# Recurrence gate blocks as Strassen pairs, and recurrence heads moved ahead of the memory gates

## The chip, the cores and the metric

The kernel runs on one core of one Trainium2 chip. The time is device microseconds of one execution, from start to end on the core. Inside a core, TensorE (PE) multiplies matrices into PSUM banks, VectorE (DVE) and ScalarE (ACT) work elementwise, GpSimd (POOL) does small elementwise work, SyncE (SP) issues the loads and stores. Each engine takes its own queue of instructions in order and waits on semaphores for the others.

## The reference, cut to what matters

One decoder layer over 512 prompt tokens and 64 sample tokens (576 columns), with model width 1024 and float32 values. A normalised input `h` is projected by `w_in`; three branches (a convolution module, a gated linear recurrence with 4 heads, a cross attention into memory) are each projected to width 1024 and merged with a sigmoid gate per channel; an output projection and an FFN follow.

```python
z = jnp.einsum('bld,de->ble', h, w_in)
ca, cb, hq, hf, hi, hgate, mq, gl = jnp.split(z, idx, axis=-1)
...
logf = jnp.log(lbh + (1.0 - lbh) * jax.nn.sigmoid(fx))          # fx: hf by heads
k = (1.0 - lbh) * jax.nn.sigmoid(-fx)
q = jax.nn.silu(hq)
o, new_hg = _hgrn2_chunkwise(q, k, v, logf, hg_state)           # 4 heads, 128 x 128 state
o = _rmsnorm(o, hg_norm_g) * jax.nn.silu(hgate)
p_hg = jnp.einsum('ble,ed->bld', o, w_hg_out)
...
g = jax.nn.sigmoid(gl.reshape(B, L, N_BRANCH, D_MODEL))
merged = g[:, :, 0] * p_conv + g[:, :, 1] * p_hg + g[:, :, 2] * p_mem
out = jnp.einsum('bld,de->ble', merged, w_out)
```

## The kernel before

Activations lie transposed: 128 channels on the partitions, 576 tokens along a row. Every float32 product is done as three matmuls on split operands (`mm3`, L95 to L97: high by high, high by low, low by high). `split` (L102, L103) makes the high part on ACT and the low part on DVE. A block of 128 output channels (`proj`) is two groups of tokens, 256 and 320 columns, with 8 contraction steps of three matmuls for each: 48 matmuls, each group in a PSUM bank of its own. The tag `mm` has four banks, the tag `sd` four more for the recurrence and other small products.

The mixer is a list of tasks, added with `add` and run in that order. Each task computes one block, and after it `pump` advances the queues of side work by some steps: `convq` (convolution) and `side` (the recurrence of a head, among others). The weights of a block are loaded and split by `wprep`, some blocks ahead (`wahead`). The code sets program order; a scheduler then places each instruction in its engine's queue by its own estimate of when operands and buffers are free, so matmuls of a block and of a head alternate on PE. Buffers of a pool are handed out in program order: the tag `tb` (`tmp`) has three, which serve the squares of a head, its output before the split, and the gates of the memory branch among others.

The blocks around the change: `gate_conv`, `gate_mem` and `gate_hg` are 8 blocks of 48 matmuls each, evicted by a sigmoid on ACT (`gate_block`, L511). `p_conv`, `p_mem` and `p_hg` are 8 blocks each of 24 matmuls, evicted on DVE with a product by the gate (`out_block`, L517 to L521). `hq` and `hf` are the projections of one recurrence head. The order in before: the gate `hgate(0)`, head 0, the other `hgate`, 8 times `p_conv`, then the memory gates and `p_mem` in turns, with head 1 after `p_mem(1)` and head 2 after `p_mem(5)`, then `gate_hg(0)`, head 3, the other `gate_hg`, and 8 times `p_hg`.

A head is a chain over four engines: `hg_decay` (scans, a reciprocal L794, scaled keys; transposes L826 and L829, copied by ACT at L827 and L830), then `hg_main` (state products L847 with L853 on DVE; scores L871 to L878; new sample states L884; outputs L887, L890, L896, L898; squares on ACT L903 and L906; their sum on DVE L904; a reciprocal root on POOL in 14 small instructions, L144 to L153; scaling on DVE L909 and L911; transposes L915 and L916; the product with the head's gate L922 and L923; the split; state updates L933).

The FFN already forms blocks of two by Strassen products in Winograd's form: it halves tokens and contraction, forms sums of token blocks and of weight blocks (`token_sums_a`, `token_sums_b`, `sprep`), and gets a block of 256 channels with 7 products (`sprod`, 4 steps of `mm3` with 288 columns) in place of 8.

## Time and profile before

| what | before |
|---|---|
| median of 3 runs | 1005.29 us (1005.02 to 1006.93) |
| profiled execution, its time | 1005.55 us |
| its span | 1003.8 us |
| TensorE granted clock, mean share of full speed | 0.997 |
| PE busy | 986.9 us, 98%, 6915 instructions |
| DVE busy | 693.3 us, 69%, 1235 instructions |
| ACT busy | 433.5 us, 43%, 766 instructions |
| POOL busy | 33.5 us, 3%, 127 instructions |

The busy shares are means over stages that differ, and the windows of the stages in question are shown below. A row of a timeline gives start and length in us, then the instruction with its line; in brackets stands the idle time of that engine ahead of it and who ended it. `x4` means four instructions of a kind in a row, with the time from the first one's start to the last one's end. A buffer's name is the tag of its pool: `wr`, `wh`, `wl` are raw, high and low weights, `tn` the small tiles of the reciprocal root.

### The profile page before, as it was taken

What the parts mean: (1) busy time and instruction counts of PE and PEld (TensorE: products, weight loads), DVE (VectorE), ACT (ScalarE), POOL (GpSimd) and SP (SyncE); (2) the same over time, 40 slices, a digit from 0 to 9 for tenths busy, and PEclk for the clock granted to TensorE, in tenths of its full rate; (3) what the DMA queues carried; (4) which work ended last, traced back from release to release, by engine and by line L of the source; (5) the groups of instructions that cost most, each with busy time, mean ns of one, the idle gap of its engine ahead of it and who ended that gap; (6) DMA issues with size and microseconds to landing.
All of it is one profiled execution on the core that took longest, in us unless ns stands there. A gap on an engine that the chain in (4) does not pass through costs nothing.

```text
span 1003.8 us, 16880 instructions
## 1 busy us (share of the span) xinstructions
PE 986.9 (98%) x6915; PEld 924.0 (92%) x6915; DVE 693.3 (69%) x1235; ACT 433.5 (43%) x766; POOL 33.5 (3%) x127
## 2 busy tenths in 40 slices
PE   8999999999899999999999999999999999999997
PEld 7997899889699999999999779999999999999995
DVE  6689997485875365566548788878777876813715
ACT  6544346574621232223234466344444544614612
POOL 1120000000101001001000000000000000000000
PEclk9999999999999999999999999999999999999999
DMA  8415421543743222222323615023232333321302
GB/s 244 140 64 194 121 80 47 148 132 107 207 134 95 84 85 75 76 87 65 95 77 134 181 64 178 1 85 114 77 104 85 96 115 137 139 81 54 128 20 95
DMA packets 125931, 106.55 MB, mean 106 GB/s; under 512 B 3208, under 2 KB 110244, under 8 KB 125846
## 3 DMA queue, kind: packets, MB, share of 16 engines
q1 hardware_dynamic: 125854, 105.48, 33.9%
q8 instruction: 54, 0.88, 0.4%
q14 instruction: 23, 0.19, 0.1%
HBM read 97.15 MB, written 8.68 MB: 105 GB/s over the span
## 4 chain that ended last, share of the span: by engine, by line
PE 82%; DVE 7%; DMA 5%; ACT 2%; issue 2%; POOL 1%; SPq 0%; DVEq 0%; ACTq 0%
PE mm L96 18%; PE mm L95 18%; PE mm L97 18%; PE sd L96 3%; PE sd L95 3%; PE sd L97 3%; PE sd L1465 2%; PE sd L1466 2%; PE sd L1467 2%; DVE wl L103 1%; DMA x<-in_cache_mem_v_dram 1%; DMA wr<-in_w_ffn_gate_dram 1%; DVE S L428 1%; DMA wr<-in_w_out_dram 1%; DVE S L106 1%
## 5 line engine op out<-in xcount | busy, mean ns | idle before, releaser
L96 PE MATMUL mm<-S,wh 128*128 128x320 f32 (+1 forms) x1216 | 363.3, 299 | 0.3 <-DVE S L106 0.3
L95 PE MATMUL mm<-S,wh 128*128 128x320 f32 (+1 forms) x1216 | 361.5, 299 | 1.5 <-ACT S L105 1.0
L97 PE MATMUL mm<-S,wl 128*128 128x320 f32 (+1 forms) x1216 | 362.4, 299 | 0.0
L95 PEld LDWEIGHTS mm<-S,wh 128*128 128x128 f32 x1216 | 227.9, 188 | 6.5 <-issue 2.6
L97 PEld LDWEIGHTS mm<-S,wl 128*128 128x128 f32 x1216 | 228.3, 188 | 3.9 <-issue 3.5
L96 PEld LDWEIGHTS mm<-S,wh 128*128 128x128 f32 x1216 | 228.6, 188 | 3.6 <-issue 1.5
L103 DVE TENSOR_TENSOR wl<-wr,wh 128x1024 fp32r<-128x1024 f32 x98 | 119.6, 1221 | 127.9 <-ACT wh L102 127.5
L102 ACT ACTIVATE wh<-wr 128x1024 fp32r<-128x1024 f32 x98 | 103.6, 1059 | 224.9 <-PE mm L96 174.1
L428 DVE SCALAR_TENSOR_TENSOR S<-S,cT,S 128x512 f32<-128x512 f32 x120 | 89.9, 749 | 2.5
L96 PE MATMUL mm<-S,wq 128*128 128x288 f32 x216 | 63.7, 295 | 0.0
L97 PE MATMUL mm<-S,wq 128*128 128x288 f32 x216 | 63.7, 295 | 0.0
L96 PE MATMUL sd<-S,wq 128*128 128x288 f32 x216 | 63.6, 295 | 0.0
L95 PE MATMUL sd<-S,wq 128*128 128x288 f32 x216 | 63.6, 294 | 0.0
L95 PE MATMUL mm<-S,wq 128*128 128x288 f32 x216 | 63.6, 294 | 0.0
L97 PE MATMUL sd<-S,wq 128*128 128x288 f32 x216 | 63.1, 294 | 0.0
L102 ACT ACTIVATE wq<-ws 128x1024 fp32r<-128x1024 f32 x36 | 37.9, 1056 | 37.8 <-PE mm L96 35.2
L103 DVE TENSOR_TENSOR wq<-ws,wq 128x1024 fp32r<-128x1024 f32 x36 | 43.7, 1217 | 3.0 <-ACT wq L102 3.0
L103 DVE TENSOR_TENSOR S<-S,S 128x1152 fp32r<-128x1152 f32 (+3 forms) x46 | 44.1, 986 | 1.8 <-ACT S L102 1.7
L102 ACT ACTIVATE S<-S 128x1152 fp32r<-128x1152 f32 (+3 forms) x46 | 38.1, 864 | 6.9 <-DVE S L521 4.9
L97 PEld LDWEIGHTS mm<-S,wq 128*128 128x128 f32 x216 | 40.6, 188 | 0.0
L96 PEld LDWEIGHTS sd<-S,wq 128*128 128x128 f32 x216 | 40.5, 188 | 0.0
L95 PEld LDWEIGHTS sd<-S,wq 128*128 128x128 f32 x216 | 40.5, 188 | 0.0
(371 smaller groups left out, 1689.5 us busy)
## 6 DMA issues: line engine op xcount, KB each, us to landing
wr<-in_w_in_dram SPq DMA_DIRECT2D x52, 512.0 KB
wr<-in_w_ffn_down_dram SPq DMA_DIRECT2D x22, 512.0 KB
S<-in_w_ffn_gate_dram SPq DMA_DIRECT2D x9, 1024.0 KB
S<-in_w_ffn_up_dram SPq DMA_DIRECT2D x9, 1024.0 KB
x<-in_x_prompt_dram SPq DMA_DIRECT2D x8, 512.0 KB
wr<-in_w_mem_kv_dram SPq DMA_DIRECT2D x8, 512.0 KB
x<-in_cache_mem_k_dram SPq DMA_DIRECT2D x8, 512.0 KB
x<-in_cache_mem_v_dram SPq DMA_DIRECT2D x8, 512.0 KB
```

The source lines that it names most:

```text
L95: T.matmul(out, lhsT=whi, rhs=xhi, start=start, stop=False, skip_group_check=more)
L96: T.matmul(out, lhsT=whi, rhs=xlo, start=False, stop=False, skip_group_check=more)
L97: last["mm"] = T.matmul(out, lhsT=wlo, rhs=xhi, start=False, stop=stop, skip_group_check=more)
L102: A.activation(hi, src, AF.Copy)
L103: (eng or V).tensor_tensor(lo, src, f32(hi), op=ALU.subtract)
L106: ins2 = V.scalar_tensor_tensor(out=lo, in0=src, scalar=scale, in1=f32(hi), op0=ALU.mult, op1=ALU.subtract)
L428: queue(V.scalar_tensor_tensor(out=dp, in0=src, scalar=w, in1=dp, op0=ALU.mult, op1=ALU.add))
L1465: T.matmul(pa[ti], lhsT=ah, rhs=w[0][:, kk, :], start=f == 0, stop=False)
L1466: T.matmul(pa[ti], lhsT=al, rhs=w[0][:, kk, :], start=False, stop=False)
L1467: T.matmul(pa[ti], lhsT=ah, rhs=w[1][:, kk, :], start=False, stop=f == NF - 1)
```

## The change

There are three parts.

1. The eight `gate_hg` blocks become four pairs. A pair takes 7 products of 12 matmuls of 288 columns, and its weights come in one load of 1 MB with `sprep` (one split of 512 columns, four sums of 512, three splits of 1024). The token sums are formed once in `token_sums`: two additions of 2304 columns, four of 1152, four splits of 1152. The results of a pair are put together from held products (`hold_` on ACT, three per pair), three instructions of DVE and sigmoids on ACT.
2. The heads move. Head 1 stands ahead of `p_conv(0)`, head 2 after `p_conv(3)`, head 3 between `gate_mem(1)` and `p_mem(0)`. `token_sums` follows `p_mem(3)`, the first weights of the pairs (`first_sums`) follow `gate_mem(7)`, the four pairs and then `p_hg` end the list.
3. `hg_alloc` takes one large tile for all heads. Heads 1 and 3 keep `z`, `kx` and `q` in the convolution buffer `ca`.

The helpers of the FFN (`half`, `token_sums_a`, `token_sums_b`, `sprep`, `sprod`, `hold_`) move up in the code and take their operands as arguments; the FFN's work is the same as before. The diff, cut to its core:

```diff
     def hg_alloc(j):
-        s1, d = big(), {}
-        for i, key in enumerate(("z", "P", "R", "iP", "kx", "qT", "sc", "q")):
+        if j == 0:
+            hg["s1"] = big()
+        s1, d = hg["s1"], {}
+        for i, key in enumerate(("P", "R", "iP", "qT", "sc")):
             d[key] = s1[:, NT * i:NT * i + NT]
+        for i, key in enumerate(("z", "kx", "q")):
+            d[key] = ca[:, i] if j % 2 else s1[:, NT * (5 + i):NT * (6 + i)]
...
+    def token_sums_a(act, r):
+        hi, lo = (x[:, :, TH[0]] for x in act)
+        V.tensor_tensor(r[:, :, TH[0]], f32(hi), f32(lo), op=ALU.add)
...
+    def token_sums_b(x):
+        r = x["r"]
+        hi, lo = (a[:, :, TH[1]] for a in x["act"])
+        V.tensor_tensor(r[:, :, TH[1]], f32(hi), f32(lo), op=ALU.add)
+        b11, b12, b21, b22 = (r[:, 4 * k:4 * k + 4, TH[t]] for k in range(2) for t in range(2))
+        V.tensor_tensor(b11, b11, b12, op=ALU.subtract)
+        split(*x["T"][0], b11)
+        V.scalar_tensor_tensor(out=b12, in0=b12, scalar=-1.0, in1=b22, op0=ALU.mult, op1=ALU.add)
+        V.scalar_tensor_tensor(out=b22, in0=b22, scalar=-1.0, in1=b11, op0=ALU.mult, op1=ALU.subtract)
+        split(*x["T"][1], b22)
+        split(*x["T"][2], b12)
+        V.scalar_tensor_tensor(out=b21, in0=b22, scalar=-1.0, in1=b21, op0=ALU.mult, op1=ALU.subtract)
+        split(*x["T"][3], b21)
...
+    def gmul(key, x, nxt, g):
+        d = sw.pop(key)
+        act, T4 = x["act"], x["T"]
+        X, Z, Y = mmb(), sdb(), sdb()
+        sprod(X, d["a"], half(act, 0, 0), True)
+        c1 = hold_(X)
+        next(nxt, None)
+        sprod(Z, d["cd"], T4[0], True)
+        c5 = hold_(Z)
+        next(nxt, None)
+        sprod(X, d["acd"], T4[1], False)
+        u2 = hold_(X)
+        sprod(Y, d["b"], half(act, 1, 0), True)
+        V.tensor_tensor(g[:, 0, TH[0]], Y[:, :HT], c1, op=ALU.add)
...
-    def gate_hg(n):
+    def gprep(p):
+        c = C_GL + D + 256 * p
+        return sprep(p, w_in[0][:, c:c + 256], gring)
+
+    def token_sums():
+        wahead(3)
+        drain(side)
+        gring["t"] = big()
+        gx.update(token_sums_a(h, gring["t"].rearrange("p (k t) -> p k t", k=8)))
+        token_sums_b(gx)
+
+    def first_sums():
+        wahead(1)
+        for _ in gprep(0):
+            pass
+
+    def gates_hg(p):
...
+            nxt = gprep(p + 1) if p < 3 else iter(())
...
+            gmul(p, gx, nxt, G1["all"][:, 2 * p:2 * p + 2])
...
+    hf(1)
     for n in range(8):
         add(p_conv(n), *([wcols(w_conv_out, P * n, 256)] if n % 2 == 0 else []), conv=2, ns=3)
+        if n == 3:
+            hf(2)
     for n in range(0, 8, 2):
         add(gate_mem(n), win(C_GL + 2 * D + P * n), ns=4)
         add(gate_mem(n + 1), win(C_GL + 2 * D + P * n + P), ns=4)
+        if n == 0:
+            hf(3)
+        if n == 6:
+            add(first_sums, ns=0)
         add(p_mem(n), wcols(w_mem_out, P * n, 256), ns=3)
         add(p_mem(n + 1), ns=3)
-        if n == 0:
-            hf(1)
-        if n == 4:
-            hf(2)
+        if n == 2:
+            add(token_sums, ns=0)
+    for p in range(4):
+        add(gates_hg(p), ns=0)
     for n in range(8):
-        add(gate_hg(n), win(C_GL + D + P * n), ns=3)
-        if n == 0:
-            hf(3)
-    for n in range(8):
-        add(p_hg(n), *([wcols(w_hg_out, P * n, 256)] if n % 2 == 0 else []))
+        add(p_hg(n))
```

The lines of a head lie 6 further down in the changed kernel: L826 is L832 there, L898 is L904, L904 is L910, L909 is L915, L915 is L921.

Three places of the new order follow. The first is the third head on PE. Before, from its output products (L887) to its last transposes (L915), with the matmuls of two `gate_hg` blocks (`mm_4732` to `mm_4817`) between; rows of the same kind are left out:

```order
L887 MATMUL sd_4596<-S_1142,S_4279 64x128
L890 MATMUL sd_4596<-x_4508,qpad 32x128 x8
L896 MATMUL sd_4606<-S_1142,S_4279 128x128 x2
L898 MATMUL sd_4606<-S_1142,S_4279 128x128
...
L96 MATMUL mm_4732<-S_114,wh_4567 128x256
L97 MATMUL mm_4732<-S_113,wl_4568 128x256
L95 MATMUL mm_4757<-S_113,wh_4567 128x320
...
L915 MATMUL sd_4678<-ident,S_4279 128x128 x4
L916 MATMUL sd_4679<-ident,S_4279 128x64
```

And after, where `mm_4062` is the last block of `gate_mem(1)` and `mm_4096` the first of `hq(3)`:

```order
L97 MATMUL mm_4062<-S_113,wl_3890 128x320
L832 MATMUL sd_3765<-ident,S_2747 128x128 x4
...
L893 MATMUL sd_3848<-S_1142,S_2747 64x128
L896 MATMUL sd_3848<-x_3819,qpad 32x128 x8
L902 MATMUL sd_3893<-S_1142,S_2747 128x128 x2
L904 MATMUL sd_3893<-S_1142,S_2747 128x128
...
L921 MATMUL sd_3927<-ident,S_2747 128x128 x4
L922 MATMUL sd_3928<-ident,S_2747 128x64
L95 MATMUL mm_4096<-S_113,wh_4032 128x256
```

About 70 matmuls of blocks stood between the output products and the last transposes; now none does, nor between the first transposes and the last.

The second is ACT around the same head. Before, from the copy of the transposes (L827) to the first eviction behind the squares:

```order
L827 ACTIVATE S_4279<-sd_4483 128x512
L830 ACTIVATE S_1142<-sd_4489 64x128
L102 ACTIVATE wh_4786<-wr_4784 128x1024
L511 ACTIVATE tb_4512<-mm_4513 128x256
L511 ACTIVATE tb_4512<-mm_4538 128x320
L903 ACTIVATE tb_4616<-sd_4606 128x512
L906 ACTIVATE tb_4619,tn_4614<-sd_4596 64x128
L511 ACTIVATE S_4731<-mm_4732 128x256
```

After, where `mm_3978` to `mm_4062` are the four banks of `gate_mem(0)` and `gate_mem(1)`:

```order
L102 ACTIVATE wh_4152<-wr_4150 128x1024
L833 ACTIVATE S_2747<-sd_3765 128x512
L836 ACTIVATE S_1142<-sd_3771 64x128
L909 ACTIVATE tb_3903<-sd_3893 128x512
L912 ACTIVATE tb_3906,tn_3901<-sd_3848 64x128
L511 ACTIVATE tb_3977<-mm_3978 128x256
L511 ACTIVATE tb_3977<-mm_4003 128x320
L511 ACTIVATE tb_4036<-mm_4037 128x256
L511 ACTIVATE tb_4036<-mm_4062 128x320
```

The evictions of the gate blocks stood ahead of the head's squares; now four of them stand behind.

The third is DVE in the last head. Before, from the last state update to the product with the gate:

```order
L933 SCALAR_TENSOR_TENSOR x_5076<-x_5076,S_4790,sd_5102 128x128
L904 TENSOR_REDUCE tn_5181<-tb_5183 128x4
L909 TENSOR_TENSOR S_4790<-sd_5173,tn_5189 128x512
L911 TENSOR_SCALAR S_4790<-sd_5105,tn_5189 64x128
L103 TENSOR_TENSOR wl_5399<-wr_5396,wh_5398 128x1024
L922 SCALAR_TENSOR_TENSOR tb_5214<-sd_5207,cT,S_183 128x512
```

After, where `S_4622` holds the token sums:

```order
L939 SCALAR_TENSOR_TENSOR x_4334<-x_4334,S_2747,sd_4360 128x128
L957 TENSOR_TENSOR S_4622<-S_113,S_114 128x8x288
L964 TENSOR_TENSOR S_4622<-S_113,S_114 128x8x288
L910 TENSOR_REDUCE tn_4440<-tb_4442 128x4
L103 TENSOR_TENSOR wl_4619<-wr_4616,wh_4618 128x1024
L966 TENSOR_TENSOR S_4622<-S_4622 128x4x288
L968 SCALAR_TENSOR_TENSOR S_4622<-S_4622 128x4x288
L915 TENSOR_TENSOR S_2747<-sd_4432,tn_4448 128x512
L917 TENSOR_SCALAR S_183<-sd_4363,tn_4448 64x128
L969 SCALAR_TENSOR_TENSOR S_4622<-S_4622 128x4x288
L928 SCALAR_TENSOR_TENSOR tb_4473<-sd_4466,cT,S_183 128x512
```

Two additions of 2304 columns now stand ahead of the reduction, and a weight split and two token sums between it and the scaling.

## Rows read from the trace of the kernel before

**Rows 1.** Windows: length, busy us of PE, PEld, DVE, ACT, POOL, clock, DMA

```profile
286.00:520.00 234.00, 234.00 (x1808) 223.36 (x1806) 129.53 (x244) 58.64 (x106) 16.71 (x64) 1.00 0.26 80
325.00:350.00 25.00, 25.00 (x191) 25.00 (x190) 8.35 (x14) 6.08 (x10) 0.00 (x0) 1.00 0.28 85
640.00:850.00 210.00, 210.00 (x1585) 210.00 (x1585) 166.75 (x253) 99.19 (x155) 0.00 (x0) 1.00 0.29 95
371.10:396.65 25.55, 25.55 (x207) 23.13 (x206) 13.21 (x31) 5.52 (x12) 3.86 (x15) 1.00 0.29 86
```

**Rows 2.** Windows, second head, PE alone, matmuls into tile mm

```profile
371.10:396.65 25.55, 16.51 (x119) 1.00 0.29 86
```

**Rows 3.** Timeline of PE, second head: start, length, instruction, idle before

```profile
371.10 0.63 PE L826 MATMUL sd<-ident,S 128*128 128x128 f32 x4
...
374.86 1.06 PE L847 MATMUL sd<-S,S 128*128 128x128 f32 x8
...
379.10 0.33 PE L878 MATMUL sd<-S 128*64 128x64 f32 x2
...
382.17 1.13 PE L884 MATMUL sd<-tb,S 32*128 32x512 f32 x4
...
386.02 0.39 PE L898 MATMUL sd<-S,S 128*128 128x128 f32 x2
...
396.06 0.60 PE L915 MATMUL sd<-ident,S 128*128 128x128 f32 x4
```

**Rows 4.** Timeline of ACT, second head

```profile
371.76 0.60 ACT L827 ACTIVATE S<-sd 128x512 f32<-128x512 f32 x1 [2.76 <-PE sd L826]
...
374.91 1.06 ACT L102 ACTIVATE wh<-wr 128x1024 fp32r<-128x1024 f32 x1 [2.25 <-PE mm L96]
...
375.99 0.71 ACT L511 ACTIVATE tb<-mm 128x256 f32<-128x256 f32 x2
...
386.45 0.60 ACT L903 ACTIVATE tb<-sd 128x512 f32<-128x512 f32 x1 [9.74 <-PE sd L898]
```

**Rows 5.** Timeline of DVE, last head

```profile
500.50 0.69 DVE L904 TENSOR_REDUCE tn<-tb 128x4 f32<-128x512 f32 x1 [0.28 <-ACT tb L903]
505.20 0.69 DVE L909 TENSOR_TENSOR S<-sd,tn 128x512 f32<-128x512 f32 x1 [4.02 <-POOL tn L153]
```

**Rows 6.** Groups of DVE, 286 to 520: busy, mean ns | idle before

```profile
L794 DVE RECIPROCAL S<-S 128x576 f32<-128x576 f32 x3 | 11.2, 3725 | 0.0
...
L796 DVE SCALAR_TENSOR_TENSOR S<-S,omlb 128x576 f32<-128x576 f32 x3 | 2.4, 814 | 0.0
...
L922 DVE SCALAR_TENSOR_TENSOR tb<-sd,cT,S 128x512 f32<-128x512 f32 x4 | 3.0, 751 | 7.6 <-PE sd L915 7.6
```

**Rows 7.** Groups of DVE, 605 to 620 us: an addition of 2304 columns

```profile
L1223 DVE TENSOR_TENSOR S<-S,S 128x2304 f32<-128x2304 f32 x1 | 2.5, 2547 | 0.0
```

**Rows 8.** Groups of DVE and ACT, 640 to 860: pieces of 1152 columns

```profile
L103 DVE TENSOR_TENSOR S<-S,S 128x1152 fp32r<-128x1152 f32 x5 | 6.6, 1354 | 0.6 <-ACT S L102 0.6
...
L102 ACT ACTIVATE S<-S 128x1152 fp32r<-128x1152 f32 x6 | 6.6, 1155 | 0.2 <-DVE wq L103 0.2
```

**Rows 9.** Timeline of POOL and DVE, third head

```profile
452.26 1.23 DVE L103 TENSOR_TENSOR wl<-wr,wh 128x1024 fp32r<-128x1024 f32 x1 [3.37 <-ACT wh L102]
...
452.37 1.17 POOL L152 TENSOR_SCALAR tn<-tn 128x5 f32<-128x5 f32 x1
```

**Rows 10.** Chain that ended last: start, length, a load of weights

```profile
558.88 6.28 DMA wr<-in_w_ffn_gate_dram
```

**Rows 11.** Windows around the one drop of the clock, columns as in 1

```profile
256.00:258.20 2.20, 0.95 (x5) 0.59 (x4) 0.89 (x4) 2.20 (x7) 0.00 (x0) 1.00 0.16 48
258.20:262.00 3.80, 3.08 (x48) 2.49 (x52) 3.80 (x10) 3.24 (x5) 0.00 (x0) 0.67 0.39 119
262.00:266.00 4.00, 3.02 (x43) 2.30 (x36) 3.96 (x9) 4.00 (x9) 0.00 (x0) 0.88 1.14 318
```

More of the change, by code (lines that the diff above doesn't have):

```diff
@@ new lines, in sprod, with hold_ @@
+    def sprod(ps, w, x, start):
+        for k in range(4):
+            mm3(ps[:, :HT], w[0][:, k], w[1][:, k], x[0][:, k], x[1][:, k], start and k == 0, k == 3, not start)
+    def hold_(ps):
+        t = tmp(HT)
+        A.activation(t, ps[:, :HT], AF.Copy)
+        return t
+    def gmul(key, x, nxt, g):
[12 more added lines that the diff above has]
+        V.tensor_tensor(g[:, 0, TH[0]], Y[:, :HT], c1, op=ALU.add)
+        next(nxt, None)
+        sprod(X, d["ac"], T4[2], False)
+        o = g[:, 1, TH[1]]
+        V.scalar_tensor_tensor(out=o, in0=X[:, :HT], scalar=-1.0, in1=c5, op0=ALU.mult, op1=ALU.subtract)
+        A.activation(o, o, AF.Sigmoid)
+        next(nxt, None)
+        sprod(Z, d["abcd"], half(act, 1, 1), False)
+        V.tensor_tensor(g[:, 0, TH[1]], Z[:, :HT], u2, op=ALU.add)
+        A.activation(g[:, 0], g[:, 0], AF.Sigmoid)
+        next(nxt, None)
+        sprod(X, d["d"], T4[3], False)
+        A.activation(g[:, 1, TH[0]], X[:, :HT], AF.Sigmoid, scale=-1.0)
@@ L1288, in sprod @@
-    def sprod(ps, w, x, start):
-        for k in range(4):
-            mm3(ps[:, :HT], w[0][:, k], w[1][:, k], x[0][:, k], x[1][:, k], start and k == 0, k == 3, not start)
     def smul(m, nxt):
@@ L1295, in smul @@
         d = sw.pop(m)
-        T4 = [tuple(x[:, i] for x in xT["hl"]) for i in range(4)]
+        T4 = xT["T"]
         h0, h1 = hid(2 * p), hid(2 * p + 1)
@@ L1318, in smul @@
         u2 = hold_(X)
[L1319 removed]
+        sprod(Y, d["b"], half(h2, 1, 0), True)
         V.tensor_tensor(o0, Y[:, :HT], c1, op=ALU.add)
```

143 lines of the change are left out of this document (63 added, 80 removed).

## The prediction

> **What bounds the kernel now.** I read the busy shares first, then windows cut to the stretches that the change touches, then the timeline of one recurrence head on each engine. TensorE (PE) is the bound: between 286 and 520 us, where the memory gates, the recurrence heads and the gate_hg blocks lie, it is busy for 234.00 us of 234.00, while VectorE (DVE) is at 129.53 and ScalarE (ACT) at 58.64 [rows 1]. So there is no idle time that the new order could win back there. What can be won is PE work, and what can be lost is cover: a head is a chain over PE, ACT, DVE and GpSimd (POOL), and in the program of before PE fills each pause of that chain with matmuls of gate blocks and projections. In the second head's window of 25.55 us, 119 of PE's matmuls belong to such blocks [rows 2], so the pauses cost nothing. The question is whether the pauses are still filled.
>
> **The products: less PE work.** Eight gate blocks of 48 matmuls (24 of 256 columns, 24 of 320) are 384; four pairs of 7 products of 4 steps of 3 matmuls, 288 columns each, are 336. So 48 go. A matmul costs 25.00 / 191 = 131 ns in a stretch of plain blocks, whose mean is 288 columns, and 210.00 / 1585 = 132 ns in the stage that already uses such products in the FFN [rows 1]. The gain is 48 x 0.131 = **-6.3 us**, and it needs PE to be the bound in the new stage too. The FFN stage says that it is: PE is busy for 210.00 us of 210.00 and DVE for 166.75 with more work per pair than here [rows 1]. A pair of gates takes PE 84 x 0.132 = 11.1 us; DVE's splits, sums and three additions per pair come to less, since the FFN's also multiply the two branches. I take the added DVE and ACT work of the pairs at nothing, covered by these products; rival B prices the loss of that cover. ScalarE's sigmoid work stays about as it was.
>
> **A head without filler.** The second head in the trace gives the steps of the chain. Transposes begin at 371.10, and ACT's copy of 0.60 begins 0.66 later [rows 3, 4]. A split of 1.06 [rows 4] can stand ahead of the copy; I count about two thirds of it, and the first product L847 is ready 1.95 us after the start. L847 to the end of L878 is 379.43 - 374.86 = 4.6 us, less a little overlap 4.45, so 6.4. L884 to the end of L898 is 386.41 - 382.17 = 4.24 [rows 3], with a handover 10.8. Squares on ACT 0.60 [rows 4], 11.45; then the reduction on DVE, the reciprocal root on POOL and the scaling on DVE, which in the last head of before run from 500.50 to 505.89: 5.39, of which DVE waits 4.02 for POOL [rows 5]. That is 16.85; the transposes L915 and L916 add 0.55 [rows 3], 17.4 us in all. How much of a head does PE cost before? The window of 25.55 us less 119 matmuls of 0.131 (15.6): 10.0 us [rows 1, 2].
>
> **The third head: +7.4.** In the new order its PE rows, from the transposes to L922, stand in one piece with no projection among them; the next matmul is the first of the block hq(3). What keeps other blocks away is that the evictions of gate_mem(0) and gate_mem(1) on ACT, which free the four banks that hq(3) needs, stand behind this head's squares. So the chain is bare: 17.4 - 10.0 = +7.4. The evictions after the squares take 0.71 for two [rows 4] and end long before the chain, so they add nothing. If ACT has no split ahead it is 6.4, and if DVE still has weight parts in its queue it is more; 5 to 10.
>
> **The fourth head: +12.5.** Here 48 matmuls of p_mem(2) and p_mem(3) stand inside the chain (6.3 us). PE reaches the end of them at 6.4 + 4.24 + 6.3 = 16.9. DVE is done with the state updates and an eviction at about 13.9 and then has the two token sums of 2304 columns, which now stand ahead of the reduction L910: 2 x 2.55 [rows 7], 19.0. Reduction 0.69, 19.7. Then 4.70 from the rows of the reduction chain [rows 5], 24.4, if POOL isn't held. While POOL works, DVE runs a weight split of 1.23 [rows 9] and two sums of 1152 columns of about 1.35 each [rows 8]. In before one POOL instruction beside such a split lasts 1.17 instead of 0.20 [rows 9]. With three DVE instructions there, 0 to 3.3 us may be lost; I take 2, since some fall between POOL's own instructions: 26.4. The two last transposes end at 27.0. The first product of gate_mem(4) waits for a bank whose eviction on ACT stands behind the first token split, which needs those transposes done: 1.16 [rows 8] and 0.4 [rows 4], 28.6 with handovers 28.8. Less the 6.3 of filler and the 10.0 that a head cost before: **+12.5**, bounds 5 to 16.
>
> The Trainium skill has a rule on that POOL row: by its page "SBUF — State Buffer", section "Who interferes with whom", a DVE instruction with two SBUF inputs contends with a GpSimd instruction that reads SBUF, and the later one is blocked until the first ends. The trace agrees in kind: one POOL instruction takes 0.97 longer beside a split of 1.23. Taken to the letter, POOL would stand still through all three DVE instructions, and the sum would be 1.3 us higher than with my 2.
>
> **The second head: +2.6.** It now stands beside p_conv. Its decay steps on DVE (a product with the previous head's output 0.75 and its tail, a reciprocal 3.73, two more steps of 0.75 and 0.81, four small ones some 0.8 by estimate) are queued ahead of the addition that frees a bank of p_conv(1), which p_conv(3) needs. That is 6.8, with the eviction 0.49 more, against three groups of 12 matmuls, 4.7 us, that PE can still do [rows 1, 6]. 6.8 + 0.5 - 4.7 = 2.6; 0 if DVE is ahead of PE at that point, 6 if it is behind.
>
> **First weights of the gates: +2.** A raw block of 1 MB is loaded and its split stands on ACT ahead of evictions of gate_mem(4) and (5). A wait for a block half that size is 6.28 at its worst [rows 10]; the load here starts early, so I take 2, from 0 to 6.
>
> **The clock: +3.** In before the one deep drop of PE's clock follows a rest: PE is busy 0.95 us of 2.20, and in the next 3.80 and 4.00 us the granted clock is 0.67 and 0.88 of 2.4 GHz, with its lower level, 1.2 GHz, in between [rows 11]. Lost: 0.33 x 3.8 + 0.12 x 4.0 = 1.7 us. The bare chains of the third and fourth head have rests of 4 to 10 us, so two such drops: 3.4, of which some falls in the wait itself; 3, from 0 to 3.4.
>
> **Sum.** -6.3 + 2.6 + 7.4 + 12.5 + 2 + 3 = +21.2 us. The profiled execution took 1005.55 us with a span of 1003.8, and the median of the runs is 1005.29, so the two agree to 0.3 us: 1005.3 + 21.2 gives **1026** us (1026.5, rounded down).
>
> **Rivals.**
>
> A, faster. Only the removed matmuls count. The place is the third and fourth head: the chains would have to overlap other PE work after all, as every head does in before (25.55 us with PE busy throughout [rows 1]). It decides if the waits of all three heads add up to less than 6.3 us, which asks the third head's chain to be near 11 us instead of 17.4 and the fourth's to be hidden by p_mem. Against it: the rows of POOL and DVE alone are 5.39 [rows 5] and PE has nothing between. 1005.3 - 6.3 = **999**. Chance 0.05. With waits that just cancel the gain, 1005: 0.04.
>
> C, short waits. The token sums cost nothing since DVE is early enough or the squares late, POOL isn't held, nothing waits for raw weights, and the clock stays. The fourth head then has its reduction at 13.9 + 0.7, 19.3 with the rest of that chain, 19.9 with the transposes, 21.4 with the split and eviction: 21.4 - 16.3 = 5.1. -6.3 + 2.6 + 7.4 + 5.1 = 8.8, **1014**. [...] Against it: DVE takes its queue in order, and the sums are in front. Chance 0.13.
>
> B, DVE becomes the bound. Token sums (2 x 2.55), four sums and four low-part splits of 1152 columns (8 x 1.35) are 15.9 us [rows 7, 8] that come in one burst, with the weight splits of gate_mem(4) to (7) and of the first pair behind. If PE also waits for a low part behind it, the 6 or so us that 48 matmuls of gate_mem cover must be taken from 15.9: about 10 more, **1036**. For it: DVE is at 52% in the stretch of the heads before the heads are pushed together [rows 1]. Against: most of the burst is already in the fourth head's term. Chance 0.08.
>
> The forecast itself has 0.70.
>
> **Range and chances.** The bounds of the forecast's own terms run from 1011 (third 5, fourth 5, the rest near nothing but 2) to over 1040 (all at once, unlikely); C lies inside the low part, B at the top. Leaving A, the cancelling case and the far ends out, 1011 to 1038 should hold 8 in 10. A measurement of this kernel can tell about 0.2%, 2 us, from no change. Faster by more than that: 0.05. Within: 0.04. Slower: 0.91.
>
> **What would show it.** Right: a window on the third head with no gate or projection matmul for some 17 us and PE idle for more than 6 of them, released by DVE and POOL; one on the fourth with PE idle for about 10, in whose DVE rows the two sums of 2.55 stand ahead of the reduction; clock windows under 1.00 right behind both; the four pairs at 11 us each with PE full. Wrong: PE busy throughout the heads (A), POOL instructions at 0.20 beside the sums (the term of 2 falls), idle of PE put down to low parts of weights (B), or pairs that take well over 11 us.

## The result, and the profile after

| | before | after |
|---|---|---|
| median | 1005.15 us (1004.26 to 1006.93, 4 runs) | 1028.55 us (1025.83 to 1029.18, 4 runs) |
| profiled execution, its time | 1005.55 us | 1025.83 us |
| its span | 1003.8 us | 1024.0 us |
| granted clock, mean | 0.997 | 0.986 |

The ratio is 1.0225, 95% interval 1.0202 to 1.0248: the change made the kernel slower by 23.4 us. 1026 was forecast, with 1011 to 1038 as its range. The profiled execution is the fastest of the four, 2.7 us under the median; the other three have a mean clock of 0.981.

The page of the kernel after, its span, part 1 (PE's busy time) and part 2 (PE's busy tenths and clock in 40 slices):

```profile
span 1024.0 us, 16857 instructions
...
PE 984.6 (96%) x6867; PEld 921.4 (90%) x6867; DVE 729.1 (71%) x1281; ACT 448.0 (44%) x786; POOL 38.5 (4%) x127
...
PE   8999999999899997959999999999999999999997
...
PEclk9999999999999998979999999999999999999999
```

PE has 48 instructions fewer and is busy for 984.6 us instead of 986.9, yet the span is 20.2 us longer. Idle time has grown from 16.9 to 39.4 us. It lies in slices 16 and 18 (384 to 410 and 435 to 461 us), and there the clock falls too.

The waits of PE in the kernel after (who waits, for whom, total us, times, longest):

```profile
PE sd L921 <- DVE S L915: 16.7, 2, 10.6
PE mm L95 <- DVE S L517: 2.5, 1, 2.5
...
PE sd L853 <- ACT S L833: 1.9, 2, 1.0
...
PE mm L95 <- ACT tb L511: 1.3, 1, 1.3
```

These four lines are 22.4 us, as much as the idle time has grown, and none of them is there before. They are the third head's and the fourth's wait for the scaling (6.13 and 10.59), the second head's bank (2.5), two waits for the copy of the transposes, and the fourth head's eviction.

Windows of the kernel after, columns as in [rows 1]: the third head, the fourth head with its way to gate_mem(4), two stretches behind the rests, and a stretch of the pairs (the first product of a pair stands at 496.16):

```profile
374.80:392.80 18.00, 10.89 (x90) 7.90 (x88) 9.38 (x24) 3.98 (x10) 3.34 (x15) 0.87 0.20 63
425.70:456.30 30.60, 17.80 (x139) 14.30 (x137) 22.08 (x34) 5.97 (x12) 5.97 (x14) 0.84 0.21 65
390.00:397.00 7.00, 5.61 (x31) 5.16 (x32) 2.64 (x5) 0.74 (x2) 0.44 (x3) 0.64 0.00 0
453.00:463.00 10.00, 8.14 (x44) 7.65 (x45) 10.00 (x15) 5.88 (x8) 0.00 (x0) 0.65 0.15 45
492.00:537.00 45.00, 45.00 (x340) 45.00 (x339) 26.19 (x39) 19.11 (x32) 0.00 (x0) 1.00 0.31 100
```

A head was 25.55 us with PE busy throughout [rows 1]. Now the third takes 18.00 with 10.89 us of PE work and hardly any block in it, and the fourth 30.60 with 17.80. Behind each rest the clock is 0.64 and 0.65. In the pairs PE is full, with 45.00 / 340 = 132 ns per matmul, and DVE is at 26.19 of 45: the cover that the prediction took for the pairs holds.

The third head on PE after, to be read against [rows 3]: its first transposes, the first state product, the last output products and the last transposes:

```profile
374.73 0.60 PE L832 MATMUL sd<-ident,S 128*128 128x128 f32 x4
...
376.43 1.16 PE L853 MATMUL sd<-S,S 128*128 128x128 f32 x8 [0.99 <-ACT S L833]
...
384.88 0.39 PE L904 MATMUL sd<-S,S 128*128 128x128 f32 x2
391.39 1.11 PE L921 MATMUL sd<-ident,S 128*128 128x128 f32 x4 [6.13 <-DVE S L915]
```

From the first transpose to the end of the last one at 392.81 it is 18.1 us; the prediction worked out 17.4. The last transposes take 1.11 us at the lower clock of 1.2 GHz instead of 0.60.

ACT evicts the four banks of gate_mem(0) and gate_mem(1) right behind this head's squares:

```profile
386.18 1.32 ACT L511 ACTIVATE tb<-mm 128x256 f32<-128x256 f32 x4
```

The banks that hq(3) needs are therefore free by 387.50, while PE waits until 391.39. In this stretch nothing that the trace shows keeps the block matmuls back but the order of PE's own queue, with the last transposes ahead of hq(3).

The fourth head on PE after:

```profile
425.73 0.60 PE L832 MATMUL sd<-ident,S 128*128 128x128 f32 x4
...
427.38 1.16 PE L853 MATMUL sd<-S,S 128*128 128x128 f32 x8 [0.94 <-ACT S L833]
...
453.58 1.09 PE L921 MATMUL sd<-ident,S 128*128 128x128 f32 x4 [10.59 <-DVE S L915]
...
456.24 0.58 PE L95 MATMUL mm<-S,wh 128*128 128x256 f32 x1 [1.28 <-ACT tb L511]
```

From 425.73 to the first product of gate_mem(4) at 456.24 it is 30.5 us, 28.8 in the prediction.

DVE in the fourth head, from the two token sums to the scaling, to be read against [rows 5]:

```profile
439.90 2.55 DVE L957 TENSOR_TENSOR S<-S,S 128x2304 f32<-128x2304 f32 x1
442.37 2.55 DVE L964 TENSOR_TENSOR S<-S,S 128x2304 f32<-128x2304 f32 x1
444.84 0.68 DVE L910 TENSOR_REDUCE tn<-tb 128x4 f32<-128x512 f32 x1
445.43 1.21 DVE L103 TENSOR_TENSOR wl<-wr,wh 128x1024 fp32r<-128x1024 f32 x1
446.57 1.35 DVE L966 TENSOR_TENSOR S<-S 128x1152 f32<-128x1152 f32 x1
447.95 1.36 DVE L968 SCALAR_TENSOR_TENSOR S<-S 128x1152 f32<-128x1152 f32 x1
452.75 0.69 DVE L915 TENSOR_TENSOR S<-sd,tn 128x512 f32<-128x512 f32 x1 [3.44 <-POOL tn L153]
```

The two additions L957 and L964 stand ahead of the reduction L910, which starts 4.4 us after the squares that it needs are done (440.44). From the reduction's start to the scaling's it takes 7.91 us; in [rows 5] it was 4.70. The reason is on POOL, in the same stretch:

```profile
445.68 2.30 POOL L144 TENSOR_SCALAR tn<-tn 128x5 f32<-128x5 f32 x1 [32.48 <-DVE tn L910]
448.06 1.31 POOL L145 TENSOR_SCALAR tn<-tn 128x5 int32<-128x5 int32 x1
449.44 0.20 POOL L150 TENSOR_TENSOR tn<-tn 128x5 f32<-128x5 f32 x1
```

L144 lasts 2.30 us instead of 0.20. It outlasts DVE's weight split, which ends at 446.64 when the first small sum has already begun, and ends at 447.98, just behind that sum (447.92) and 0.03 us after the second one has begun. L145 lasts 1.31 and ends with the second sum (449.31). From then on every instruction takes 0.20. POOL has lost 3.2 us.

### The profile page after: what moved, and what is told of

It reads as the page before. It is cut to its first block, busy times and chain, and to the rows that moved or that the text cites. A ratio compares the mean times of both kernels' runs of the same rounds, so it can differ in the third digit from the quotient of the medians.

```text
span 1024.0 us, 16857 instructions
## 1 busy us (share of the span) xinstructions
PE 984.6 (96%) x6867; PEld 921.4 (90%) x6867; DVE 729.1 (71%) x1281; ACT 448.0 (44%) x786; POOL 38.5 (4%) x127
## 4 chain that ended last, share of the span: by engine, by line
PE 83%; DVE 8%; ACT 3%; POOL 2%; issue 2%; DMA 2%; DVEq 0%; SPq 0%; POOLq 0%; ACTq 0%
PE mm L95 18%; PE mm L96 18%; PE mm L97 18%; PE sd L96 3%; PE sd L97 3%; PE sd L95 3%; PE sd L1528 2%; PE sd L1529 2%; PE sd L1530 2%; DVE wl L103 1%; DVE S L428 1%; PE mm L743 1%; PE mm L742 1%; PE mm L741 1%; DVE S L106 1%
## 5 line engine op out<-in xcount | busy, mean ns | idle before, releaser
L95 PE MATMUL mm<-S,wh 128*128 128x320 f32 (+1 forms) x1088 | 325.8, 302 | 5.0 <-DVE S L517 2.5
L96 PE MATMUL mm<-S,wh 128*128 128x320 f32 (+1 forms) x1088 | 327.3, 301 | 0.3 <-DVE S L106 0.3
L97 PE MATMUL mm<-S,wl 128*128 128x320 f32 (+1 forms) x1088 | 326.1, 301 | 0.0
L95 PEld LDWEIGHTS mm<-S,wh 128*128 128x128 f32 x1088 | 206.0, 190 | 9.6 <-DVE S L517 2.7
L96 PEld LDWEIGHTS mm<-S,wh 128*128 128x128 f32 x1088 | 206.6, 190 | 4.9 <-issue 3.0
L97 PEld LDWEIGHTS mm<-S,wl 128*128 128x128 f32 x1088 | 206.2, 190 | 3.2 <-issue 2.7
L103 DVE TENSOR_TENSOR wl<-wr,wh 128x1024 fp32r<-128x1024 f32 x90 | 109.8, 1221 | 96.3 <-ACT wh L102 96.0
L96 PE MATMUL mm<-S,wq 128*128 128x288 f32 x264 | 77.9, 295 | 0.0
L97 PE MATMUL mm<-S,wq 128*128 128x288 f32 x264 | 77.8, 295 | 0.0
L96 PE MATMUL sd<-S,wq 128*128 128x288 f32 x264 | 77.8, 295 | 0.0
L95 PE MATMUL sd<-S,wq 128*128 128x288 f32 x264 | 77.7, 294 | 0.0
L95 PE MATMUL mm<-S,wq 128*128 128x288 f32 x264 | 77.7, 294 | 0.0
L97 PE MATMUL sd<-S,wq 128*128 128x288 f32 x264 | 77.2, 294 | 0.0
L103 DVE TENSOR_TENSOR wq<-ws,wq 128x1024 fp32r<-128x1024 f32 x44 | 53.5, 1219 | 9.1 <-ACT wq L102 8.9
L103 DVE TENSOR_TENSOR S<-S,S 128x1152 fp32r<-128x1152 f32 (+3 forms) x50 | 49.3, 1014 | 2.8 <-ACT S L102 2.8
L97 PEld LDWEIGHTS mm<-S,wq 128*128 128x128 f32 x264 | 49.6, 188 | 0.0
L96 PEld LDWEIGHTS sd<-S,wq 128*128 128x128 f32 x264 | 49.5, 188 | 0.0
L95 PEld LDWEIGHTS sd<-S,wq 128*128 128x128 f32 x264 | 49.5, 188 | 0.0
L96 PEld LDWEIGHTS mm<-S,wq 128*128 128x128 f32 x264 | 49.6, 188 | 0.0
## 6 DMA issues: line engine op xcount, KB each, us to landing
S<-in_w_ffn_gate_dram SPq DMA_DIRECT2D x9, 1024.0 KB
S<-in_w_ffn_up_dram SPq DMA_DIRECT2D x9, 1024.0 KB
```

The lines of the kernel that those rows point to most:

```text
L95: T.matmul(out, lhsT=whi, rhs=xhi, start=start, stop=False, skip_group_check=more)
L96: T.matmul(out, lhsT=whi, rhs=xlo, start=False, stop=False, skip_group_check=more)
L97: last["mm"] = T.matmul(out, lhsT=wlo, rhs=xhi, start=False, stop=stop, skip_group_check=more)
L103: (eng or V).tensor_tensor(lo, src, f32(hi), op=ALU.subtract)
```

## The experiments

The theory: the loss is made by head chains that PE has nothing to run beside (third and fourth head), by the token sums ahead of the last head's reduction, by POOL held up by DVE, and by the slower clock behind each rest; the pairs themselves are worth their 48 matmuls. The rivals: the pairs with their sums are what costs, or DVE is the bound and will make PE wait wherever the work stands.

| run | time, us | ratio to before (95%) |
|---|---|---|
| kernel after | 1028.55 | 1.0225 (1.0202 to 1.0248) |
| e1_og_in_place | 1005.73 | 1.0004 (0.9995 to 1.0014) |
| e2_sums_after_scaling | 1019.49 | 1.0142 (1.0127 to 1.0157) |
| e3_plain_gates | 1027.04 | 1.0219 (1.0204 to 1.0234) |
| e4_pairs_spread_heads | 1009.67 | 1.0045 (1.0030 to 1.0060) |
| e5_all_filled | 1002.22 | 0.9964 (0.9955 to 0.9974) |
| e6_filler_in_rests | 1026.2 | 1.0207 (1.0192 to 1.0221) |
| e7_small_sums_after_scaling | 1024.7 | 1.0193 (1.0178 to 1.0207) |
| e8_filled_plain_gates | 1008.15 | 1.0028 (1.0016 to 1.0040) |
| e9_head1_behind_p_conv | 1008.02 | 1.0026 (1.0017 to 1.0036) |
| e10_heads_close_behind_p_conv | 1014.74 | 1.0099 (1.0084 to 1.0115) |

### e1: the output written over its gate

The buffers of the tag `tb` are handed out in program order, and there are three. A head's output sits in one until its split, and the split waits for the large tile that `p_conv(7)` frees last. So, in program order, the outputs of heads 0 and 1 leave one buffer for the squares of head 2 and the evictions of the memory gates. The edit writes the output over the gate that it is multiplied with:

```diff
         gt = gates[:, j]
-        og = tmp()
+        og = gt
```

> One edit in the changed kernel: the product of a head's output with its gate is written over the gate instead of into a buffer of the tag tb, so the outputs of heads 0 and 1 no longer hold two of the three tb buffers until p_conv(7), and the evictions of gate_mem(0) and (1) need not wait for head 2. PE's order then has 57 block matmuls inside the third head and 141 inside the fourth. Theory (the loss is the bare chains, and their cause is the three tb buffers): the waits of 6.1 and 10.6 us before the last transposes go, the eviction wait of 1.3 and the slow clock behind both (about 4) with them: 1028.5 - 22 = 1006, between 1002 and 1009. Rival (DVE is the bound over the packed heads and the token sums, so PE only waits elsewhere, at evictions and low parts of weights): 1015 or more, with DVE near full between 430 and 470 us.

It gave 1005.73 us. The waits of PE on the same lines (columns as above):

```profile
PE mm L95 <- DVE S L517: 2.5, 1, 2.5
PE sd L853 <- ACT S L833: 1.9, 2, 1.0
...
PE mm L95 <- ACT tb L511: 1.2, 1, 1.2
```

The waits for the scaling are gone from both heads, with nothing else changed in the program's text; 22.8 us come back. DVE does the same work as in the kernel after (727.4 us busy) and doesn't make PE wait anywhere new by more than a microsecond, so the rival of DVE as the bound falls. The bare chains were the loss, and the use of the three buffers decides whether they are bare.

How it decides is another matter than the expectation had it. ACT and PE in e1's third head, and POOL in its fourth:

```profile
387.04 0.60 ACT L909 ACTIVATE tb<-sd 128x512 f32<-128x512 f32 x1 [8.63 <-PE sd L904]
...
387.78 1.28 ACT L511 ACTIVATE tb<-mm 128x256 f32<-128x256 f32 x4
```

```profile
388.20 0.39 PE L95 MATMUL mm<-S,wh 128*128 128x256 f32 x1 [1.20 <-ACT tb L511]
```

```profile
441.46 4.47 POOL L150 TENSOR_TENSOR tn<-tn 128x5 f32<-128x5 f32 x1
```

The four evictions stand behind the head's squares (L909) in e1 too, and cost 1.2 us there; this is the third line of the waits, a new one, and the fourth head's eviction wait is gone. What differs is PE's queue: hq(3) stands ahead of the last transposes, 57 block matmuls from 388.20 to 395.74. Nor were the buffers held in the run of the kernel after: ACT split the outputs of heads 0 and 1 at 363.07 to 364.31 and DVE at 367.43 to 368.84, long before head 2's squares at 385.30. So the buffers act on the order that the scheduler gives the queues. By which of its estimates they do so no run shows. In the fourth head POOL is held up even longer than in the kernel after, 4.47 us in one instruction, and the token sums still stand ahead of the reduction; with 141 block matmuls inside the head PE doesn't wait for either.

### e2 and e3: the sums' place, and what the pairs themselves cost

e2 keeps the changed order but lets the token sums start only behind the last head's scaling:

```diff
+        last["scaled"] = V.tensor_scalar(d["ons"][:64, :], obs[:64, :P], r[:64, 4:5], None, op0=ALU.mult)
 ...
-        gx.update(token_sums_a(h, gring["t"].rearrange("p (k t) -> p k t", k=8)))
-        token_sums_b(gx)
+        with tc.issue_after(last["scaled"].ins):
+            gx.update(token_sums_a(h, gring["t"].rearrange("p (k t) -> p k t", k=8)))
+            token_sums_b(gx)
```

> One edit in the changed kernel: the token sums may start only after the last head's scaling (L917), so the reduction L910 and the reciprocal root on POOL stand ahead of them. Theory (the two additions of 2.55 and the blocking of POOL by DVE cost the fourth head 5.1 + 3.2 us): PE's wait before the last transposes falls from 10.6 to about 2.5, the eviction wait of 1.3 behind it goes too, and the third head stays bare: 1028.5 - 9 = 1019.5, between 1017 and 1022. Rival (the sums are a burst of 16 us on DVE whose place doesn't matter, since behind the head they hold up the evictions of gate_mem(4) and (5) as long): 1026 or more, with new PE waits on L520 or on low parts of weights.

e3 keeps the places of the heads, with the plain gates:

```diff
-        if n == 6:
-            add(first_sums, ns=0)
...
-        if n == 2:
-            add(token_sums, ns=0)
-    for p in range(4):
-        add(gates_hg(p), ns=0)
     for n in range(8):
...
+        add(gate_hg(n), win(C_GL + D + P * n), ns=3)
...
```

> The heads stand as in the changed kernel, but the gate_hg blocks are the eight plain ones of before: no token sums, no pairs. PE's order has the third head bare, and 48 block matmuls in the fourth, as in the changed kernel. Theory (what costs is where the heads stand): against the changed kernel +6.3 for 48 more matmuls, -9.5 in the fourth head (5.1 + 3.2 + 1.3), about -1 for a shorter rest's clock: 1024, between 1021 and 1027. Rival (the pairs with their sums are what costs, and moved heads are nearly free): 1005 to 1009.

e2 gave 1019.49 us. PE's waits for the scaling in e2:

```profile
PE sd L921 <- DVE S L915: 10.1, 2, 6.1
```

The third head's wait is still 6.1; the fourth's fell from 10.6 to 4.0, not to 2.5 as expected, since a weight split still held POOL up once and the squares came 0.5 us after the state updates. The burst of sums behind the head cost PE one wait of 1.3 us.

e3 gave 1027.04, 3 us above the middle of what was expected and at the very top of its range. Its line of waits for the scaling is the same as e2's, 10.1 us over both heads. Two steps of the expectation failed: the fourth head's wait is 4.0 as in e2, not about 2.5, and the clock cost more than in the kernel after, not less. PE is busy for 993.7 us, 6.8 more than before with the same 6915 matmuls; the kernel after lost 4.0 that way (below).

So without any token sums or pairs the moved heads cost 10.1 us of waits here, and e3 is 7.5 us above e2, which has the pairs. Part of that is the clock: from 285 to 380 us, around the second head, it is 0.98 in e3 and 1.00 in e2, and in the same 91.6 us of busy time PE does 704 and 716 matmuls, which is 1.6 us; e2's wait of 1.3 goes the other way. The pairs gain; the places of the heads lose.

### e4: spread heads were not enough

e4 spreads the heads over p_conv and the memory gates, and keeps the token sums free to start:

```diff
-    hf(1)
     for n in range(8):
         add(p_conv(n), *([wcols(w_conv_out, P * n, 256)] if n % 2 == 0 else []), conv=2, ns=3)
-        if n == 3:
-            hf(2)
+    hf(1)
     for n in range(0, 8, 2):
 ...
-        if n == 0:
-            hf(3)
 ...
         add(p_mem(n + 1), ns=3)
-        if n == 2:
+        if n == 0:
+            hf(2)
+        if n == 2:
+            hf(3)
+        if n == 4:
             add(token_sums, ns=0)
```

> The Strassen pairs as in the changed kernel, but the heads spread apart: head 1 after p_conv(7), head 2 after p_mem(1), head 3 after p_mem(3), the token sums after p_mem(5). PE's order has 110 to 125 block matmuls inside each of the four heads; the token sums still stand ahead of the last head's reduction. Theory (the pairs are worth 48 matmuls, -6.3 us, and only bare chains spend it): 999, between 997 and 1001.5. Rival (a pair's sums, held products and loads cost PE as much as the 48 matmuls, or the token sums delay DVE for whatever stands there): 1004 to 1010.

It gave 1009.67, and the expectation of 999 was wrong. The waits of PE:

```profile
PE sd L921 <- DVE S L915: 3.6, 1, 3.6
PE mm L95 <- ACT tb L511: 3.4, 1, 3.4
```

Three of the four heads are free of waits. The last one stands with the token sums, and its 3.6 and 3.4 us come although 74 block matmuls lie behind its output products: the two additions are ahead of the reduction, three small sums hold POOL up behind it (1.16, 1.31 and 1.31 us for one instruction each), and three token splits of 3.27 us on ACT stand ahead of an eviction. That is the second half of the rival, the token sums delay what stands behind them; the expectation had put down only the bare chains. The two waits are 7.0 of the 10.7 us above 999; besides, PE is busy for 984.6 us, 5.0 more than in e5 (below) with the same products, at a mean clock of 0.990 against 0.996.

### e5 and e8: everything covered, with pairs and without

e5 spreads the heads, writes the output over the gate (as e1) and holds the sums back (as e2), with some 190 block matmuls between the last head and the first pair:

```diff
-    hf(1)
     for n in range(8):
         add(p_conv(n), *([wcols(w_conv_out, P * n, 256)] if n % 2 == 0 else []), conv=2, ns=3)
-        if n == 3:
-            hf(2)
+        if n == 1:
+            hf(1)
+    hf(2)
     for n in range(0, 8, 2):
 ...
-        if n == 0:
-            hf(3)
 ...
         add(p_mem(n + 1), ns=3)
+        if n == 0:
+            hf(3)
```

> The changed kernel with three edits: the heads spread (head 1 after p_conv(1), head 2 after p_conv(7), head 3 after gate_mem(1) and p_mem(1)), the head's output written over its gate, and the token sums only after the last head's scaling. PE's order has 94 to 127 block matmuls inside every head, and 194 between the last head's end and the first pair. Theory (bare chains, the sums ahead of the reduction, and the sums too close to the first pair are all that spends the 48 matmuls): PE waits for nothing in the stretch and the time is 1005.3 - 6.3 = 999, between 998 and 1001. Rival (DVE's added 36 us of work must show up somewhere): 1003 or more.

e8 is e5's order with plain gates and no sums, the edits of e5 and of e3 together:

```diff
-        if n == 6:
-            add(first_sums, ns=0)
...
-        if n == 2:
-            add(token_sums, ns=0)
-    for p in range(4):
-        add(gates_hg(p), ns=0)
     for n in range(8):
...
+        add(gate_hg(n), win(C_GL + D + P * n), ns=3)
...
```

> The order of e5 (heads spread and filled, output over its gate), but with the eight plain gate_hg blocks of before and no token sums. Theory (48 matmuls are the whole worth of the pairs, and filled heads cost nothing): as before, 1005, between 1004 and 1006.5, and 6.3 above e5. Rival (the spread order itself wins or loses some us beside the pairs): outside of 1003 to 1007.

e5 gave 1002.22 us, ratio 0.9964 (0.9955 to 0.9974): it is 3.3 us under before, not 6.3, and just outside the range that was expected. A window of e5 from the last head through the token sums into the pairs (columns as in [rows 1]), and its waits in the stretch:

```profile
445.00:505.00 60.00, 60.00 (x452) 59.77 (x451) 52.10 (x72) 30.14 (x44) 0.00 (x0) 1.00 0.30 97
```

```profile
PE mm L95 <- DVE S L517: 1.4, 1, 1.4
...
PE mm L95 <- DVE mt L520: 1.0, 1, 1.0
PE sd L853 <- ACT S L833: 1.0, 1, 1.0
```

DVE is at 52.10 of 60 us there and PE still full. What is missing are small waits: 1.4 us where head 1's decay steps stand ahead of an eviction of p_conv, 1.0 and 1.0 elsewhere. e8 gave 1008.15, out of the range that was expected, 2.6 us above before. It has two of the three waits, 1.4 and 1.0 (the third belongs to the pairs' sums). So the spread order itself costs some 2.5 us, and the pairs gain 1008.15 - 1002.22 = 5.9 us beside it.

### e6: dummy work in the rests

```diff
         pT, pTs = sdb(), sdb()
+        if j >= 2:
+            fill(pTs[:, P:2 * P], (0, 0, 50, 88)[j])
         for t in range(4):
```

> The changed kernel with 50 dummy transposes of 128x128 on PE ahead of the last transposes of the third head and 88 ahead of the fourth's, about as long as PE's rests there; their results aren't used and they feed nothing. Theory (the rests let PE's clock fall to 1.2 GHz, which costs about 4 us behind them): the granted clock stays near 1.00 in 390 to 397 and 453 to 463 and the time is 1028.5 - 4 = 1024.5, between 1023 and 1026. Rival (the slow clock costs nothing that counts, or transposes don't hold the clock up): 1027.5 or more, and the clock in those windows still near 0.65.

It gave 1026.2 us, between the expected range and the rival's. The same windows (columns as in [rows 1]), and PE at the first product behind the fourth head:

```profile
390.00:397.00 7.00, 6.35 (x54) 5.88 (x53) 2.40 (x5) 0.90 (x2) 2.35 (x12) 1.00 0.08 25
453.00:463.00 10.00, 7.68 (x46) 7.14 (x45) 9.22 (x13) 6.93 (x9) 0.57 (x3) 0.83 0.16 54
```

```profile
456.82 0.38 PE L95 MATMUL mm<-S,wh 128*128 128x256 f32 x1 [1.37 <-ACT tb L511]
```

Behind the third head the clock stays at 1.00, where only 0.65 us of PE's rest are left: there the rest had lowered the clock, and work in it keeps it up. Behind the fourth the edit helped less than 0.83 against 0.65 suggests. The clock is 1.00 through the dummy transposes and the last transposes, up to 456.80, and then 0.54 up to 460.40: the first 17 block matmuls run at the lower clock, as many as in the kernel after, although PE's rests were now only 0.95 and 1.37 us. So here two short rests, with transposes between and ahead of them, were followed by the drop too; what in them brought it on is not shown. The time fell by 2.3 us where 4 was expected, and the intervals of the two runs overlap (1.0192 to 1.0221 against 1.0202 to 1.0248). What the clock costs in time is therefore read from the trace of the kernel after (below).

### e7: is POOL held up by DVE?

The two additions stay ahead of the reduction; the sums of 1152 columns wait for the scaling:

```diff
-        b11, b12, b21, b22 = ...
-        V.tensor_tensor(b11, b11, b12, op=ALU.subtract)
-        ...
+        with tc.issue_after(last["scaled"].ins):
+            b11, b12, b21, b22 = ...
+            V.tensor_tensor(b11, b11, b12, op=ALU.subtract)
+            ...
```

> The changed kernel, where the two additions of 2304 columns still stand ahead of the last head's reduction, but the sums and splits of 1152 columns start only after its scaling, so that DVE runs no sums while POOL works out the root. Theory (POOL was blocked for 3.2 us by DVE's two-input instructions): the root's 14 instructions all take 0.20 or near it save one beside a weight split, PE's wait falls from 10.6 to about 8, the time to 1025.5, between 1024 and 1027. Rival (POOL's two long instructions were a late start of something else): 1028 or more, and they stay at 2.30 and 1.31.

It gave 1024.7 us, within what was expected. All four executions are shorter than each of the kernel after, though the two intervals touch (1.0178 to 1.0207 against 1.0202 to 1.0248), so the trace decides. POOL in the last head, and DVE beside it:

```profile
446.83 1.02 POOL L144 TENSOR_SCALAR tn<-tn 128x5 f32<-128x5 f32 x1 [32.48 <-DVE tn L910]
```

```profile
445.98 0.68 DVE L910 TENSOR_REDUCE tn<-tb 128x4 f32<-128x512 f32 x1
446.58 1.22 DVE L103 TENSOR_TENSOR wl<-wr,wh 128x1024 fp32r<-128x1024 f32 x1
451.50 0.69 DVE L915 TENSOR_TENSOR S<-sd,tn 128x512 f32<-128x512 f32 x1 [3.70 <-POOL tn L153]
```

One POOL instruction is long, 1.02, and ends with the weight split (447.80); the rest take 0.20. The scaling starts 5.52 us after the reduction instead of 7.91, and PE's wait is 8.2 instead of 10.6. The blocking is real and cost 2.4 us of the fourth head beyond what the split alone costs; a wait of 1.4 on an eviction of p_mem (L520), now behind the sums, comes in place of the 1.3. e7 and e2 agree on the fourth head: e7 takes away 2.4 of its wait, e2 takes 6.6, of which the order of the additions is the larger part.

### e9 and e10: two attempts at a better order

Both drop the head beside p_conv, from e5:

```diff
-        if n == 1:
+        if n == 7:
             hf(1)
-    hf(2)
```

In the loop over the memory gates, e9 has

```diff
         add(gate_mem(n + 1), win(C_GL + 2 * D + P * n + P), ns=4)
+        if n == 2:
+            hf(3)
 ...
         add(p_mem(n + 1), ns=3)
         if n == 0:
-            hf(3)
-        if n == 2:
+            hf(2)
+        if n == 4:
             add(token_sums, ns=0)
```

and e10

```diff
         add(gate_mem(n + 1), win(C_GL + 2 * D + P * n + P), ns=4)
+        if n == 0:
+            hf(2)
```

> As e5, but with no head beside p_conv: head 1 after p_conv(7), head 2 after p_mem(1), head 3 after gate_mem(3), token sums after p_mem(5) and the last head's scaling. 100 to 130 block matmuls stand inside heads 0 to 2, 94 inside the last, 98 between its end and the first pair. Theory (what kept e5 above 999 is head 1's run of decay steps on DVE ahead of an eviction of p_conv, 1.4 us, and its clock): 1002.2 - 1.5 = 1000.7, between 999.5 and 1002, with no wait of PE on L517. Rival (the 98 matmuls ahead of the first pair are too few for the token sums, as in e4): 1003 or more, with waits of PE on ACT or DVE in the last 30 us before the pairs.

> As e9, but the heads follow each other closely: head 1 after p_conv(7), head 2 after gate_mem(1), head 3 after p_mem(1), token sums after p_mem(3) and the last head's scaling. 48 block matmuls (6.3 us) stand behind head 2's output products, 78 inside the last head, and 210 between its end and the first pair. Theory (a head's root chain of 6.1 us is just covered by 48 matmuls, and the sums have room): 1000.7, between 999.5 and 1002.5. Rival (with heads this close DVE is behind by several us, so PE waits at evictions and transposes): 1004 or more, with waits on L915 or L511.

Both were misses, with times in the rivals' ranges. e9 gave 1008.02: its waits at the first pair, and a window there:

```profile
PE mm L95 <- ACT wa L102: 3.0, 1, 3.0
...
PE mm L97 <- DVE wa L103: 1.6, 1, 1.6
```

```profile
460.00:480.00 20.00, 15.39 (x104) 14.84 (x102) 20.00 (x26) 8.12 (x10) 0.00 (x0) 0.93 0.32 105
```

The wait on p_conv's eviction is gone, but DVE is busy for 20.00 us of 20.00 and the 98 matmuls are over before the sums and the first weights are done. The 3.0 has a load in it: the raw weights of the first pair go into the tile that holds the token sums, their load starts only at 469.30, behind token splits of DVE, and ACT splits them at 474.28, where it had waited 2.25 us for them. e10 gave 1014.74. DVE and PE around the end of its third head and the start of its fourth:

```profile
424.99 3.74 DVE L800 RECIPROCAL S<-S 128x576 f32<-128x576 f32 x1
...
431.24 1.42 DVE L822 TENSOR_TENSOR S<-S,F 128x512 f32<-128x512 f32 x2
```

```profile
423.46 0.63 PE L921 MATMUL sd<-ident,S 128*128 128x128 f32 x4 [0.41 <-DVE S L915]
...
432.80 1.09 PE L832 MATMUL sd<-ident,S 128*128 128x128 f32 x4 [8.51 <-DVE S L822]
```

DVE runs the fourth head's reciprocal (L800) only at 424.99, behind the third head's last transposes at 423.46: it writes the part of the shared large tile from which these read. The scaled keys that the transposes at 432.80 need follow from 431.24 to 432.66, and PE waits 8.5 us. The waits that the rival named, on L915 and L511, are 0.4 and 1.2 there. So e9 and e10 miss for different reasons. In e9 a burst on DVE, which is not the bound in the mean, has too little PE work beside it; e5, with 194 block matmuls there, has enough. In e10 it is the third part of the change, one large tile for all heads, that ties the start of a head to the end of the one before.

## Why the prediction was right

| term | predicted, us | shown, us |
|---|---|---|
| 48 matmuls | -6.3 | -5.9 (e8 to e5), -7.5 (e3 to e2, at unequal clocks) |
| third head | +7.4 | 0.99 + 6.13 = 7.1 of waits |
| fourth head | +12.5 | 0.94 + 10.59 + 1.28 = 12.8 of waits |
| second head | +2.6 | 2.45, one wait on L517 |
| first weights | +2 | no such wait |
| clock | +3 | 4.0 in the profiled run |
| sum | +21.2 | +20.2 profiled span, +23.4 medians |

The clock's 4.0 is what PE's busy time went up by beside the products: 984.6 - 986.9 = -2.3, and -2.3 + 6.3 = 4.0. The rows behind the two rests bear it out: 11 block matmuls of 256 columns take 2.46 us from 392.73 and 17 take 3.76 from 456.24, where 0.12 each is usual, 2.9 us more, and the last transposes of the two heads 1.0 more.

**The products.** Right. PE is full in the pairs at 132 ns per matmul, and DVE and ACT are covered there.

**The third head.** Right in size, and in that the chain is bare: 18.1 us against 17.4, of which 0.5 is the lower clock in the last transposes. The reason that it gave for the bareness does not hold. It said that the evictions behind the head's squares keep hq(3) away; they were done by 387.50, and in e1, where they stand behind the squares as well, the chain is filled. PE's queue has hq(3) behind the last transposes, and the allocation of the three `tb` buffers decides that.

**The fourth head.** Right in mechanism and near in size: 30.5 us against 28.8. POOL lost 3.2 us, not 2, and the last transposes took 0.5 more at the lower clock, which the prediction had put under the clock. The step that failed is that some of the three DVE instructions would fall between POOL's own: POOL's first instruction sat behind two of them and its second behind the third one. Here the page "SBUF — State Buffer" of the Trainium skill, section "Who interferes with whom", taken to the letter as the prediction did, was nearer: blocked through all three, priced at 1.3 us more than its 2. That the reduction would start 19.0 after the first transposes held: 444.84 - 425.73 = 19.1.

**The second head.** 2.45 against 2.6; the place (L517 behind the reciprocal) is as predicted.

**First weights.** Wrong by its 2 us, and the load didn't start early: it starts at 460.42, since its tile holds the token sums until they are split, and ACT waits 3.93 us for it, up to 465.34, ahead of an eviction, as predicted. But PE is busy for 29.00 us of 29.00 from 463 to 492, and the first pair comes at 496.16, so the wait on ACT costs nothing. The bound of 6.28 was read from a chain elsewhere.

**The clock.** Mechanism right (windows at 0.64 and 0.65 behind the rests; in e6 1.00 behind the third head). The prediction's price of 1.7 us per rest came to some 2.0 in the profiled run. The other three executions are 3 us longer than the profiled one at a mean clock of 0.981 instead of 0.986, and no trace of them exists. Traces of other runs show where a clock can differ between executions: from 250 to 285 us, ahead of the change, it is 0.95 in the kernel after and 0.85 in e1, and from 285 to 380, around the second head's wait of 2.45, it is 1.00 in the kernel after and 0.98 in e1, with the same wait. By estimate from these windows two such drops would bring 0.986 down to 0.981; that the three executions had them is not shown.

**The rivals.** A, the cover in place after all, needs one edit more: e1 has it in the third and fourth head, and e5, with two further edits, is faster than before. B did not happen in the kernel after, where no wait on a low part lies in these stages; it did in e9 (1.6 us, L97 on L103). C fell: the sums were in front, as the queue said.

Against the profiled execution the sum is 1.0 too high: the first weights were 2 too high and the clock 1.0 too low, while the heads came within 0.3 each. That it also came out within 2.6 us of the median is in part luck: the medians hold some 3 us that no term of the sum had, and the 2 for the first weights made up for most of them.

## What to carry to other kernels

When work with a long chain over several engines is moved, look in the new queue of the bounding engine for what stands between the chain's first and last step; where nothing does, its whole length less its own work is paid, and the cause may be a small pool whose buffers are handed out in program order, even when no buffer is waited for in the run (e1). A burst on a second engine that is idle in the mean is free only if the first engine has as much other work right beside it, ahead of whoever needs the burst's result (e5 against e9). One tile shared between chains ties the start of one to the end of the other (e10). Fewer products were worth about their own time here, 5.9 us for 48 matmuls, so a reordering that they need must cost less than that.
